# A planner's charges for VectorE, ScalarE and GpSimd instructions, in a one-core hybrid encoder step

## The chip, the core and the metric

The kernel runs on one core of a Trainium2 chip. Its engines are TensorE (PE, with weight loads shown apart as PEld), VectorE (DVE), ScalarE (ACT), GpSimd (POOL) and SyncE (SP), which here issues all DMAs. The metric is the device time of one execution in microseconds, as a median of several runs.

## The reference, cut to what matters

One inference step of a one-layer encoder, for a prompt of 256 frames and 8 streams of 16 frames (384 tokens in all), model width 2048, all in float32:

```python
mem_k, mem_v = mem @ w_xk, mem @ w_xv
proj = x @ w_in                # diff q, k, v | DeltaNet q, k, v, z, a, b | two merge gates
o_a = diff_attention(...)      # 8 heads
o_b = gated_delta_chunked(...) # 16 heads; sol = triangular_solve(I + m, rhs) for each block
mix = sigmoid(gate_a) * (o_a @ w_pa) + sigmoid(gate_b) * (o_b @ w_pb)
h1 = LN(alpha * x + mix @ w_o)
h2 = LN(alpha * h1 + cross_attention(h1, mem_k, mem_v))
y  = LN(alpha * h2 + (silu(h2 @ w_ff1) * (h2 @ w_ff3)) @ w_ff2)
```

Outputs are `y` and the new caches and states.

## The kernel before

Each large product is a *job*: 16 weight tiles of 128 x 128, streamed from HBM in halves of eight tiles (512 KB, tile `raw`). ScalarE casts a half to a high part (`wh`), VectorE subtracts to get the low part (`wl`), and TensorE adds three matmuls of 384 columns for each weight tile into one accumulator `acc`. A job is 48 matmuls, and the stream of jobs (`Kern.stream`) runs through the whole kernel: memory keys and values, the gated-DeltaNet projections with 25 of the merge gates (150 to 1000 us), differential attention (1000 to 1490), the merge products, the output product (1780 to 1915), cross attention (to 2035) and the feed-forward part (2035 to 3170).

All other work is written as generators (tasks) that are woven between the matmuls. The order of every instruction on every engine is fixed while the program is written out, by a planner, the class `Driver`. It keeps one clock for each engine. `Driver.note` (called for each instruction that is emitted) adds a charge to that engine's clock and writes down when the outputs are due: 130 ns after the end. A task gives up control with `yield` and names what it waits for; `Driver.wake` lets it go on when all of that is due, plus a pad of 60 ns, by PE's planned clock. `Driver.poll` is called after each group of three matmuls (a quantum), and steps the ready task of the best priority, again and again, until nothing may run or PE's clock has moved by a budget of 300 ns. A task is held back while VectorE's or ScalarE's planned clock is ahead of PE's by more than its limit:

```python
ahead = max(self.clk["DVE"], self.clk["ACT"]) - self.clk["PE"]
if w is None or w > self.clk["PE"] or ahead > t.lim: continue
```

`Driver.until` blocks the stream itself: it polls, and where nothing can run, moves PE's planned clock on. `Driver.due` looks an operand up by tile and offset, and where that address was never written, by the tile's latest write.

In the gated-DeltaNet stage the heads go by in pairs (`HB` = 2), a block of ten jobs for each: three convolution jobs for each head, a gate job for each head and two z jobs of the pair before. Four lanes of tasks run beside them: `conv_silu` (evacuation, convolution taps on ScalarE and GpSimd, result `kq` or `vT`), `stage1` (priority 3, limit 1500; ends with the tile `vr`), `solve_lane` (priority 8, limit 900) and two `stage2_lane`s (priority 4, limit 1500; each head ends with `y`). `solve_lane` takes pair after pair: when stage 1 of both heads is done it loads the factors, runs 156 steps of the 64-row solve with 22 of the 16-row one in between, all single VectorE instructions on `sol_u`, gives up control after every fourth big step, and stores the result, which stage 2 loads as `uz`. A step works on 1 to 63 columns:

```python
for j in range(n - 1):
    for c in range(j // nsp + 1):
        nc.vector.scalar_tensor_tensor(out=u[:, c, j + 1:], in0=m(j), scalar=u[:, c, j:j + 1], in1=u[:, c, j + 1:], ...)
```

with `n`, `nsp` = 64, 16 for the big solve and 16, 8 for the small one. A convolution job of head h waits (`until`) for the end of stage 2 of head h - 6, a z job for that of head h - 5. After the last pair's convolutions come its two z jobs and seven gate jobs; the stage then waits for all its lanes.

Of the kernel before, what the change touches and what calls it, by code (L numbers as in the profile page):

```python
# [12 lines left out]
ALU = mybir.AluOpType  # L13
# [124 lines left out]
class Driver:  # L138
# [26 lines left out]
    def note(self, kind, op, a, k):  # L165
        aps = [v for v in list(a) + list(k.values()) if isinstance(v, bass.AP)]
        assert not any(v.name in self.dead for v in aps), (op, [v.name for v in aps])
        out = k.get("out")
        if out is None:
            out = aps[0]  # L170
        outs = [out] + ([k["accum_out"]] if k.get("accum_out") is not None else [])
        ins = [v for v in aps if not any(v is o for o in outs)]
        free = lambda v: v.size() // v.shape[0] if callable(getattr(v, "size", None)) else int(np.prod(v.shape[1:]))
        n = int(np.prod(out.shape[1:]))
        start = max([self.clk[kind]] + [self.due(v) for v in ins] + [self.ready.get(o.name, 0.0) if self.key(o) not in self.ready else 0.0 for o in outs])
        if kind != "PE":
            start = max(start, self.clk["PE"])
        lat = 130.0
        if kind == "DMA":
            nbytes = 4 * int(np.prod(out.shape))  # L180
            self.clk["DMA"] = max(self.clk["DMA"], start) + nbytes / 380.0
            fin = self.clk["DMA"] + 2300.0
        else:
            if kind == "PE":
                m = out.shape[0]
                if ins[0].dtype == F32R:
                    cost = 3 + n * 0.4167
                elif op == "transpose":
                    cost = 110.0
                else:  # L190
                    cost = max(4 * n * 0.4167, 110.0) * (1.0 if m > 64 else 0.65 if m > 32 else 0.36)
            elif kind == "DVE":
                f = 1.04
                if op == "tensor_reduce":
                    n = int(np.prod(ins[0].shape[1:]))
                elif op == "reciprocal":
                    f = 8.3
                elif op in ("tensor_copy", "tensor_scalar_mul", "tensor_scalar_add", "tensor_scalar", "memset") and all(
                        str(v.space) == "SB" for v in aps):
                    f = 0.52  # L200
                cost = 70 + n * f
            elif kind == "ACT":
                cost = 210 + n * 0.83
            else:
                cost = 150 + n * (2.2 if op == "tensor_tensor" else 1.2)
            fin = start + cost
            self.clk[kind] = fin
        for o in outs:
            self.ready[self.key(o)] = fin + lat
            self.ready[o.name] = max(self.ready.get(o.name, 0.0), fin + lat)  # L210
        for v in aps:
            self.last[v.name] = max(self.last.get(v.name, 0.0), fin + lat)
# [1884 lines left out]
```

## Time and profile before

| | us |
|---|---|
| median of 3 runs | 3198.93 |
| lowest, highest | 3197.56, 3202.95 |
| profiled execution | 3205.78 |
| its span, first to last instruction | 3204.0 |
| PE busy in the span | 3110.1 |
| DVE, ACT, POOL busy | 1828.2, 1215.0, 534.6 |

Busy times are unions: overlapping instructions of one engine count once. Matmuls are pipelined, so a busy PE need not be at its peak, and the spacing of its matmuls says more. The line number of nearly all instructions is 115, the helper that records them, so groups are told apart by their tiles.

### The profile page before, as it was taken

Reading aid. Unit: us, or ns where it says so; the run is one execution under the profiler, and the core shown is the slowest. Engines: PE = TensorE matmul, PEld = TensorE weight load, DVE = VectorE, ACT = ScalarE, POOL = GpSimd, SP = SyncE. Lnnn points to the kernel's source line nnn. Section 1 sums busy time; section 2 is a strip of 40 time slices with the busy share of each in tenths; the row PEclk is TensorE's granted clock in tenths of the full one; section 3 lists DMA queues with packets and bytes.
Section 4 is the critical chain, followed back from the end, with each engine's and each line's share of the span. In section 5 each row is a group of like instructions: output and inputs, shape, how many; then the busy total and the mean of one; then the engine's idle time right before and its main releaser. Section 6 shows DMA issues by size and latency. Waiting matters only on the chain.

```text
span 3204.0 us, 49130 instructions
## 1 busy us (share of the span) xinstructions
PE 3110.1 (97%) x18889; PEld 3045.3 (95%) x18889; DVE 1828.2 (57%) x3785; ACT 1215.0 (38%) x2122; POOL 534.6 (17%) x760
## 2 busy tenths in 40 slices
PE   8999999999999999999999998899999999999996
PEld 8999999988999999999999997799999999999996
DVE  5476778777762444444444767955554345555445
ACT  5554544544422443333223334433332223333332
POOL 0343433423310000000000334600000000000312
PEclk9999999999999999999999999999999999999998
DMA  8455544555554555455544756233334443333442
GB/s 280 137 148 164 162 138 144 160 151 154 142 155 163 165 179 192 155 172 183 165 148 150 259 193 217 96 127 123 125 125 122 125 127 126 120 127 123 122 127 81
DMA packets 190027, 486.22 MB, mean 152 GB/s; under 512 B 42832, under 2 KB 83296, under 8 KB 185696
## 3 DMA queue, kind: packets, MB, share of 16 engines
q1 hardware_dynamic: 189792, 483.08, 47.8%
q8 instruction: 148, 2.42, 0.3%
q14 instruction: 87, 0.71, 0.1%
HBM read 444.49 MB, written 38.50 MB: 151 GB/s over the span
## 4 chain that ended last, share of the span: by engine, by line
PE 84%; DVE 7%; DMA 4%; POOL 1%; issue 1%; ACT 1%; SPq 1%; ACTq 0%; DVEq 0%; POOLq 0%
PE acc L115 79%; DVE sol_u L115 3%; DVE wl L115 2%; PE ps L115 1%; PE ch L115 1%; DVE h L115 1%; PE do L115 1%; SPq L115 1%; PE dsc L115 1%; DMA sol_u<-in_u 1%; DMA sol_ma<-scr_ma 1%; POOL h L115 1%; POOL ln_s L115 1%; PE o L115 1%; DMA uz<-scr_up 1%
## 5 line engine op out<-in xcount | busy, mean ns | idle before, releaser
L115 DVE TENSOR_TENSOR wl<-raw,wh 128x1024 fp32r<-128x1024 f32 (+2 forms) x692 | 854.3, 1235 | 778.1 <-ACT wh L115 774.3
L115 ACT CAST wh<-raw 128x1024 fp32r<-128x1024 f32 (+2 forms) x692 | 719.1, 1039 | 1507.8 <-PE acc L115 1383.2
L115 PE MATMUL acc<-xh,wh 128*128 128x384 f32 x2320 | 819.5, 353 | 0.0
L115 PE MATMUL acc<-xh,wl 128*128 128x384 f32 x2320 | 781.0, 337 | 0.0
L115 PE MATMUL acc<-xl,wh 128*128 128x384 f32 x2320 | 780.2, 336 | 0.0
L115 PE MATMUL acc<-hh,wh 128*128 128x386 f32 x1472 | 504.4, 343 | 0.0
L115 PE MATMUL acc<-hh,wl 128*128 128x386 f32 x1472 | 499.0, 339 | 4.7 <-DVE wl L115 4.7
L115 PE MATMUL acc<-hl,wh 128*128 128x386 f32 x1472 | 499.6, 339 | 2.9 <-DVE hl L115 2.9
L115 PEld LDWEIGHTS acc<-xh,wh 128*128 128x128 f32 x2320 | 439.3, 189 | 13.2 <-issue 11.4
L115 PEld LDWEIGHTS acc<-xl,wh 128*128 128x128 f32 x2320 | 439.7, 190 | 1.5
L115 PEld LDWEIGHTS acc<-xh,wl 128*128 128x128 f32 x2320 | 438.1, 189 | 0.0
L115 PEld LDWEIGHTS acc<-hl,wh 128*128 128x128 f32 x1472 | 279.2, 190 | 5.1 <-DVE hl L115 4.1
L115 PEld LDWEIGHTS acc<-hh,wl 128*128 128x128 f32 x1472 | 278.4, 189 | 5.0 <-DVE wl L115 5.0
L115 PEld LDWEIGHTS acc<-hh,wh 128*128 128x128 f32 x1472 | 278.6, 189 | 1.9 <-issue 1.2
L115 PE MATMUL acc<-fh,wh 128*128 128x384 f32 x704 | 238.3, 338 | 0.0
L115 PE MATMUL acc<-fl,wh 128*128 128x384 f32 x704 | 238.0, 338 | 0.0
L115 PE MATMUL acc<-fh,wl 128*128 128x384 f32 x704 | 238.0, 338 | 0.0
L115 POOL TENSOR_TENSOR h<-h,ln_sh 128x384 f32<-128x384 f32 x30 | 39.2, 1345 | 927.3 <-ACT ln_sh L115 927.3
L115 POOL TENSOR_TENSOR cy<-cy,tap 128x408 f32<-128x408 f32 x144 | 177.4, 1232 | 53.0 <-ACT tap L115 48.8
L115 DVE SCALAR_TENSOR_TENSOR sol_u<-sol_mb,sol_u 128x31 f32<-128x31 f32 (+30 forms) x864 | 159.6, 258 | 0.0
L115 PEld LDWEIGHTS acc<-fh,wh 128*128 128x128 f32 x704 | 131.9, 187 | 0.1
L115 PEld LDWEIGHTS acc<-fl,wh 128*128 128x128 f32 x704 | 131.9, 187 | 0.1
(305 smaller groups left out, 3999.6 us busy)
## 6 DMA issues: line engine op xcount, KB each, us to landing
raw<-in_w_ff SPq DMA_DIRECT2D x240, 512.0 KB
raw<-in_w_gdn SPq DMA_DIRECT2D x128, 512.0 KB
raw<-in_w_diff SPq DMA_DIRECT2D x96, 512.0 KB
raw<-in_w_gate SPq DMA_DIRECT2D x64, 512.0 KB
raw<-in_w_pb SPq DMA_DIRECT2D x32, 512.0 KB
raw<-in_w_pa SPq DMA_DIRECT2D x32, 512.0 KB
raw<-in_w_o SPq DMA_DIRECT2D x32, 512.0 KB
raw<-in_w_ff SPq DMA_DIRECT2D x32, 384.0 KB
```

Of the source, the lines that this page charges most:

```text
L115: r = f(*a, **k)
```

## The change

`Driver.note` charges other durations for VectorE, ScalarE and GpSimd instructions. VectorE: 165 ns + 1.04 for each column, from 70 + 1.04; 0.65 a column for copies and the like within SBUF, from 0.52; the reciprocal's 8.3 a column goes. ScalarE: 150 + 0.87 a column, from 210 + 0.83, and 150 more where a sum is accumulated. GpSimd: a pow is 370 + 180 a column, another `tensor_tensor` 350 + 2.3 (both were 150 + 2.2), and the rest 200 + 1.2, from 150 + 1.2. The charges for PE and DMA stay. Every instruction stays; the order in which they are written out on each engine may differ.

```diff
                 if op == "tensor_reduce":
                     n = int(np.prod(ins[0].shape[1:]))
-                elif op == "reciprocal":
-                    f = 8.3
                 elif op in ("tensor_copy", "tensor_scalar_mul", "tensor_scalar_add", "tensor_scalar", "memset") and all(
                         str(v.space) == "SB" for v in aps):
-                    f = 0.52
-                cost = 70 + n * f
+                    f = 0.65
+                cost = 165 + n * f
             elif kind == "ACT":
-                cost = 210 + n * 0.83
+                cost = 150 + n * 0.87 + (150 if k.get("accum_out") is not None else 0)
+            elif k.get("op") == ALU.pow:
+                cost = 370 + 180 * n
             else:
-                cost = 150 + n * (2.2 if op == "tensor_tensor" else 1.2)
+                cost = 350 + n * 2.3 if op == "tensor_tensor" else 200 + n * 1.2
```

## Rows read from the trace of the kernel before

**Rows 1.** Busy by stretch (length; PE, PEld, DVE, ACT, POOL; PE clock; DMA; GB/s).

```profile
150.00:1000.00 850.00, 818.20 (x5183) 792.54 (x5182) 620.55 (x2050) 398.10 (x910) 289.14 (x498) 0.99 0.52 153
...
1900.00:2100.00 200.00, 174.24 (x1107) 158.61 (x1107) 161.77 (x254) 85.64 (x161) 95.29 (x80) 0.95 0.46 159
2100.00:3170.00 1070.00, 1070.00 (x6057) 1069.73 (x6057) 531.81 (x720) 316.97 (x358) 44.40 (x30) 1.00 0.39 122
```

**Rows 2.** Waits of PE, 150 to 1000 us (total, times, longest).

```profile
PE ps L115 <- DVE kq L115: 12.0, 7, 3.5
PE ch L115 <- DMA uz<-scr_up: 6.8, 5, 2.5
PE dtr L115 <- DVE lam L115: 4.4, 1, 4.4
```

**Rows 3.** Timeline of VectorE, 633 to 645 us (start, us, instruction; count last).

```profile
634.60 7.62 DVE L115 SCALAR_TENSOR_TENSOR sol_u<-sol_mb,sol_u 128x14 f32<-128x14 f32 x36
...
643.28 0.61 DVE L115 SCALAR_TENSOR_TENSOR kq<-pad,cy 128x256 f32<-128x256 f32 x2
```

**Rows 4.** Timeline of PE, 636 to 648 us.

```profile
639.97 0.33 PE L115 MATMUL acc<-xl,wh 128*128 128x384 f32 x1
640.14 0.34 PE L115 MATMUL acc<-xh,wl 128*128 128x384 f32 x1
643.75 0.71 PE L115 MATMUL ps<-cst_all,kq 128*128 128x128 f32 x3 [3.27 <-DVE kq L115]
...
644.58 0.52 PE L115 MATMUL acc<-xl,wh 128*128 128x384 f32 x1
644.90 0.52 PE L115 MATMUL acc<-xh,wl 128*128 128x384 f32 x1
```

**Rows 5.** Groups by shape (busy us, mean ns | idle before, releaser).

```profile
L115 DVE TENSOR_TENSOR wl<-raw,wh 128x1024 fp32r<-128x1024 f32 x656 | 820.0, 1250 | 769.3 <-ACT wh L115 768.8
...
L115 ACT CAST wh<-raw 128x1024 fp32r<-128x1024 f32 x656 | 689.8, 1051 | 1434.3 <-PE acc L115 1313.7 <-issue 95.8 <-ACT dtt L115 5.5
...
L115 POOL TENSOR_TENSOR cy<-cy,tap 128x408 f32<-128x408 f32 x144 | 177.4, 1232 | 53.0 <-ACT tap L115 48.8
...
L115 POOL TENSOR_TENSOR cols<-ssk,half 128x3 f32<-128x3 f32 x16 | 15.0, 935 | 24.7 <-DVE ssk L115 24.4
```

**Rows 6.** Stretches of the eight solves, instructions on `sol_u` alone (DVE busy, count).

```profile
188.00:273.00 85.00, 40.38 (x178) 0.98 0.41 128
297.00:368.00 71.00, 30.62 (x178) 1.00 0.40 126
400.00:464.00 64.00, 32.65 (x178) 1.00 0.42 122
484.00:556.00 72.00, 33.69 (x178) 0.98 0.45 144
575.00:650.00 75.00, 36.60 (x178) 0.98 0.45 138
673.00:747.00 74.00, 37.12 (x178) 0.98 0.44 137
776.00:851.00 75.00, 35.14 (x178) 1.00 0.44 136
881.00:930.00 49.00, 28.79 (x178) 1.00 0.44 135
```

**Rows 7.** The fifth stretch: instructions on `wl` (PE, PEld, DVE), then all.

```profile
575.00:650.00 75.00, 36.17 (x106) 20.29 (x106) 16.70 (x14) 0.98 0.45 138
...
575.00:650.00 75.00, 70.52 (x462) 67.42 (x461) 67.12 (x242) 39.49 (x100) 32.55 (x54) 0.98 0.45 138
```

**Rows 8.** Instructions of two tiles (ns min/median/max, first and last start).

```profile
L115 DVE TENSOR_TENSOR vr<-ps,cols x16: 545/554/558, 137.1 to 867.8; 128x384 f32<-128x384 f32 x16
...
L115 DVE SCALAR_TENSOR_TENSOR y<-o,gng,zg x16: 603/611/622, 327.5 to 978.9; 128x384 f32<-128x384 f32 x16
```

**Rows 9.** Timeline of VectorE, 372 to 378 us.

```profile
374.99 0.63 DVE L115 SCALAR_TENSOR_TENSOR kq<-pad,cy 128x256 f32<-128x256 f32 x2 [1.54 <-ACT pad L115]
```

## Prediction

> **What bounds the kernel now.** I read the busy time by stretch first [rows 1]. TensorE is the bound: from 2100 to 3170 us it is busy in all of 1070 us, and what the planner does there can win nothing. Only two stretches have slack: the gated-DeltaNet stage, 150 to 1000 us, where PE is busy 818.2 of 850 us (31.8 idle), and 1900 to 2100 us (normalisation and cross attention, 25.8 idle). The waits of PE in the first stretch come next [rows 2]: the largest are on `kq` (12.0 us in 7 waits), on the solved matrix `uz` (6.8 us) and on `lam` (4.4 us, once). The timeline shows how a wait on `kq` arises [rows 3, 4]: VectorE runs 36 solve steps from 634.60 on for 7.62 us, and only at 643.28 the `kq` for which PE has stood still for 3.27 us. TensorE then issues every 0.32 us instead of every 0.17 us, the lower of its two clock levels, so a long wait costs more than itself; the mean granted clock of the stretch, 0.99, allows at most about 8.5 us for that.
>
> So the stage is bound by TensorE, with VectorE (620.6 us busy of 850) close behind, and PE's stops there come from an order that expected VectorE to be further along.
>
> **What the change does to the charges.** No instruction is added or removed; every effect goes by the order that `Driver` writes out. Old charge, new charge and measured mean [rows 5]: `wl` of 1024 columns 70 + 1065 = 1135, then 165 + 1065 = 1230, measured 1250 ns; `wh` 1060, then 1041, measured 1051; GpSimd add of 408 columns 1048, then 1288, measured 1232; GpSimd pow of 3 columns 157, then 910, measured 935. ScalarE hardly moves. The extra 150 ns for `accum_out`, the reciprocal without its 8.3 (at most two or three columns each) and the 0.65 for copies within SBUF shift single tasks by tenths of a microsecond; I cost them at nothing, since the waits in rows 2 do not name them. If that cover is gone, one such chain is late by under 1 us for each head, 16 us at the very most and in either direction.
>
> The term that counts is the triangular solve: 178 VectorE steps for each pair of heads, 8 pairs, 1424 in all. Their column counts follow from `solve`: 3760 elements in 156 big steps, 148 in 22 small ones. Old charge for a pair: 178 x 70 + 1.04 x 3908 = 16.5 us. New: 178 x 165 + 1.04 x 3908 = 33.4 us. Measured: the eight busy times of rows 6 add up to 275.0, 34.4 us for a pair. So the new charge is right in occupancy and the old was half of it.
>
> [...]
>
> **Gain: PE's stops.** With VectorE's real backlog in its clock, the planner puts `kq`'s transposes, `vr`'s and `uz`'s matmuls behind more streaming matmuls. Of the 31.8 us idle, 4.4 us on `lam` is no matter of charges; the rest is 27.4, and with some 6 us of lower clock 33. I take 28 us. From 1900 to 2100 us much is chains with nothing else to run; I take 3 us of 25.8. The tail after 3170 is one chain: 0. Bounds of the gain: 0 and 45 us.
>
> **Loss: the solve gets slower in the order.** `solve_lane` runs at the lowest priority of its stage (8) and only while VectorE and ScalarE are planned at most 900 ns ahead of PE (`lim`). Doubling its charge doubles what each step fills of that allowance. All eight solves have 178 steps in windows of 85, 71, 64, 72, 75, 74, 75 and 49 us [rows 6]. In the fifth, VectorE has 242 instructions [rows 7]: 178 steps, 14 `wl` (one for every eighth group of three matmuls) and 50 others. Old charges: 16.5 + 15.9 + about 10.5 = 43 us, which is 0.57 of the 75 us. New: 33.4 + 17.2 + about 15 = 66 us, 0.87. The same window therefore holds the new plan only if the gate lets VectorE be planned 0.87 full, where it has been 0.57.
>
> How full can it get? The first solve answers. There every address of `sol_u` is new to the planner, so each step is charged from the tile's latest write plus 130 ns: 16.5 + 178 x 0.13 = 39.6 us, plus about 31 us for others (estimated at the fifth window's 26.4 us in 75, stretched to 85), 70.6 of 85 us = 0.83, with steps that cost about what the new ones cost. I take 0.865, between that 0.83 and the 0.87 to 0.9 at which nothing would change. The others take 32/75 = 0.43, so a later solve needs 33.4 / (0.865 - 0.43) = 77 us (83 at 0.83, 71 at 0.90) instead of 72 on average. The first has (33.4 + 23.1) / 0.435 = 130 us; TensorE comes to wait for it, which frees VectorE, and I take 125 instead of 85.
>
> The lane is a chain: solve, store, load of the next pair, solve. Between the windows of rows 6 lie 19 to 32 us; I take 21 us, near the least, where the next factors have long been there. The last solve then starts at 188 + 125 + 6 x 77 + 7 x 21 = 922 us; now it is about 881, 14 us after its pair's first part ends at 867.8 [rows 8]: the lane has no lateness left there now, and would have then. From its start to the last `y` at 978.9 [rows 8] it now takes 98 us. PE's other work (two z jobs and seven gates) would end near 979 - 28 = 951, after which nothing competes, so I take 40 us for the last solve, 8 for its store and load and 35 for the chain behind it: 922 + 83 = 1005, against 979. That is +26 us, with the stops that vanish already in it. In between, `conv_job` of heads 6 and 7 waits for the end of heads 0 and 1: the first `y` is at 327.5 [rows 8], the convolution of head 6 reaches VectorE at 374.99 [rows 9], some 20 us after its job begins, so about 28 us of slack meet 40 us of delay. TensorE stops for some 12 us there, which is not on the path as long as the last chain ends later.
>
> **Sum.** The profiled execution took 3205.8 us (span 3204.0). 3205.8 + 26 - 3 = 3228.8; it lies 6.9 us above the median of 3198.9, so the forecast on the median's scale is 3222 us.
>
> **Rivals.** *A, the lane keeps up* (0.33): planned occupancy 0.90 or more, because bigger steps leave a bigger reserve on VectorE while small matmuls push PE's clock ahead. Then T = 70, the first solve 110: last start 865, end 865 + 50 + 49 = 964, 15 us earlier than now, with the 3 us from cross attention 3181 us; a lane with no lateness at all gives 3171. It decides from about 74 us for a solve on, since each microsecond there counts six times. For it: 0.83 is already reached with holes; against it: the fifth window has 0.57. *B, the forecast* (0.45): 3222, from 3200 at T = 74 to 3250 at T = 84 with the first solve at 140, where the formula gives +83 us, of which I keep about 50 since waiting TensorE lets the lane run. *C, the lane starves* (0.10): occupancy rises to only 0.70, T = 33.4 / 0.27 = 124 us; every block then waits in `conv_job`; with the lane quick in each wait I reckon some 18 us for each of six blocks, about 3305. *D, the order hardly changes* (0.12): PE's own charges, untouched, set most of the order, and small gains and losses cancel: 3199 within 10 us.
>
> **How the numbers follow.** A measurement of this kernel can tell about 0.2% (6.4 us) from no change. Faster: 0.31 of A and 0.04 of D, 0.35. Same: 0.02 of A, 0.05 of B, 0.06 of D, 0.13. Slower: 0.40 of B, 0.10 of C, 0.02 of D, 0.52. The range goes from 3168 (below it a lane without lateness and nearly all idle time gone, 0.09) to 3285 (above it most of C, 0.09). B alone would be 3200 to 3250. Both signs hold much of the chance, and the point is B's.
>
> **What would show it.** Right: no run of over 20 solve steps between two `wl`, PE's waits on `kq` under 3 us together, and a first solve of over 110 us; windows of 75 us or more for the solves after it, the last solve starting after 900 us, and PE idle between about 950 and the end of the stage. Wrong: windows of 70 us or less, or a last solve that still starts 14 us after its pair's first part; then the gain is all that is left and A holds. PE stops of tens of microseconds ahead of a convolution job would show C. Unchanged waits on `kq` would show D. From 2100 to 3170 us nothing should move by more than 1 us.

## The result and the profile after

The changed kernel takes 3269.92 us (median of 6 runs, 3267.16 to 3273.27) against 3199.68 us before, a ratio of 1.022 [1.0209, 1.0231]: 70 us slower. The forecast was 23 us slower. Its profiled span is 3271.5 us.

Where the time went, by the windows view of the kernel after (length; PE, PEld, DVE, ACT, POOL busy with counts; PE clock; DMA share; GB/s):

```profile
150.00:1060.00 910.00, 835.56 (x5143) 806.17 (x5142) 625.82 (x2049) 396.82 (x909) 285.70 (x496) 0.95 0.48 142
...
1970.00:2170.00 200.00, 175.63 (x1106) 162.12 (x1105) 161.74 (x254) 85.34 (x160) 89.34 (x79) 0.92 0.46 160
2170.00:3240.00 1070.00, 1070.00 (x6057) 1069.73 (x6056) 530.38 (x719) 316.74 (x357) 44.43 (x30) 1.00 0.39 122
```

The last two lines answer the last two of [rows 1]: nearly the same busy times, 70 us later. All of the difference lies in the DeltaNet stage. TensorE's first matmul behind that stage starts at 1052.88 us instead of 986.05, and from there to the end the two traces agree within about 1 us. In the stage TensorE is idle for 74.4 us where it was idle for 31.8 [rows 1]: +42.6 of the +66.8 us. The other 24 us are in busy time. The granted clock is 0.95 where it was 0.99, and where it is 0.50 the stream's matmuls come 0.32 us apart instead of 0.17 [rows 4]; how much of the 24 us that makes was not taken apart.

PE's waits from 150 to 1060 us (total, times, longest), the answer to [rows 2]:

```profile
PE ch L115 <- DMA uz<-scr_up: 28.2, 3, 20.3
PE o L115 <- DVE y L115: 15.4, 7, 3.0
PE ch L115 <- DVE vr L115: 7.6, 13, 1.0
PE ch L115 <- issue: 6.0, 7, 1.4
PE o L115 <- DVE sol_u L115: 5.0, 1, 5.0
```

No wait on `kq` is left in that list; it was the largest before, 12.0 us. Instead TensorE waits for what stands behind a solve: `uz` (6.8 before), then the links of the stage-2 chain, `y` and `vr`.

The stretches of the eight solves, instructions on `sol_u` alone (DVE busy, count), the answer to [rows 6]:

```profile
190.30:342.30 152.00, 43.67 (x178) 1.00 0.44 139
363.00:450.10 87.10, 36.95 (x178) 0.96 0.36 112
471.70:536.50 64.80, 36.17 (x178) 0.95 0.39 124
560.20:620.90 60.70, 32.02 (x178) 0.94 0.40 124
643.40:764.00 120.60, 40.80 (x178) 1.00 0.44 136
791.50:856.50 65.00, 36.13 (x178) 0.95 0.38 123
879.60:949.40 69.80, 28.65 (x178) 0.95 0.43 136
973.70:1019.60 45.90, 27.91 (x178) 0.80 0.34 104
```

The first and the fifth take 152 and 121 us (85 and 75 before), at a clock of 1.00: TensorE streams on while the lane creeps. Then the stream reaches a convolution job (once a z job) whose buffer needs an earlier pair's stage 2, stops, and the lane runs quickly. The first of these stops, at the convolution of head 6, on PE's timeline:

```profile
342.90 0.34 PE L115 MATMUL acc<-xh,wl 128*128 128x384 f32 x1
...
371.66 0.67 PE L115 MATMUL acc<-xh,wh 128*128 128x384 f32 x1
```

In between, for 28.8 us, no matmul of the stream starts; in the kernel before, the longest such stop in the stage is 5.2 us. TensorE is idle for 12.2 us of it, as the chain's own matmuls run there. Where TensorE stops, all instructions (same columns as the first view):

```profile
340.00:350.00 10.00, 3.48 (x20) 3.19 (x19) 3.96 (x11) 1.44 (x2) 0.00 (x0) 0.80 0.53 145
463.00:485.00 22.00, 14.29 (x123) 10.34 (x121) 16.30 (x82) 5.49 (x24) 1.14 (x3) 0.92 0.59 160
579.00:594.00 15.00, 8.04 (x97) 5.97 (x96) 14.87 (x80) 4.20 (x19) 1.53 (x2) 0.93 0.31 86
782.00:805.00 23.00, 14.63 (x127) 11.13 (x126) 17.15 (x86) 5.58 (x24) 2.04 (x7) 0.89 0.62 159
912.00:918.00 6.00, 2.98 (x31) 1.99 (x35) 6.00 (x25) 0.88 (x3) 0.00 (x0) 0.84 0.39 116
995.00:1048.00 53.00, 20.28 (x171) 15.12 (x171) 29.69 (x160) 6.99 (x31) 5.77 (x14) 0.66 0.21 59
```

Of these 129 us TensorE is idle for 65.3, in the last stretch for 32.7: nothing competes with the last chain any more, as the timeline of PE shows (start, us, instruction; in brackets the wait ahead of it):

```profile
1004.91 0.87 PE L115 MATMUL o<-cst_all,y 128*128 128x128 f32 x3 [4.95 <-DVE sol_u L115]
1026.07 0.77 PE L115 MATMUL ch<-vr,uz 128*128 128x128 f32 x2 [20.29 <-DMA uz<-scr_up]
...
1047.25 0.87 PE L115 MATMUL o<-cst_all,y 128*128 128x128 f32 x3 [2.72 <-DVE y L115]
1047.78 0.67 PE L115 MATMUL acc<-xh,wh 128*128 128x384 f32 x1
1048.24 0.52 PE L115 MATMUL acc<-xl,wh 128*128 128x384 f32 x1
1048.56 0.52 PE L115 MATMUL acc<-xh,wl 128*128 128x384 f32 x1
...
1052.88 0.56 PE L115 MATMUL dtr<-lam,cst_all 128*128 128x2 f32 x2 [2.83 <-DVE lam L115]
```

After the stop the matmuls are 0.32 us apart, at a granted clock of 0.50 (1047.5 to 1052 us), as in [rows 4], where it is 0.50 from 644 to 647 us and 1.00 again from 648 on. The two tiles of [rows 8], after:

```profile
L115 DVE TENSOR_TENSOR vr<-ps,cols x16: 539/551/558, 142.2 to 897.7; 128x384 f32<-128x384 f32 x16
L115 DVE SCALAR_TENSOR_TENSOR y<-o,gng,zg x16: 603/617/619, 371.1 to 1048.2; 128x384 f32<-128x384 f32 x16
```

Stage 1 ends at 897.7 and the last solve starts 76 us later, at 973.7; before it was 14 us.

### The profile page after: what moved, and what is told of

The parts are those of the page before. It is cut to its first block, busy times and chain, and to the rows that moved or that the text cites. A ratio compares the mean times of both kernels' runs of the same rounds, so it can differ in the third digit from the quotient of the medians.

```text
span 3271.5 us, 49139 instructions
## 1 busy us (share of the span) xinstructions
PE 3137.3 (96%) x18889; PEld 3070.5 (94%) x18889; DVE 1836.9 (56%) x3785; ACT 1214.5 (37%) x2122; POOL 526.5 (16%) x760
## 4 chain that ended last, share of the span: by engine, by line
PE 64%; DVE 2%; DMA 1%; issue 0%; ACT 0%; POOL 0%; SPq 0%; ACTq 0%; DVEq 0%; POOLq 0%
PE acc L115 61%; PE do L115 1%; PE dsc L115 1%; DVE h L115 1%; PE fb L115 0%; DMA rawx<-scr_ob 0%; DVE wl L115 0%; PE xss L115 0%; DVE ln_s L115 0%; DVE lu L115 0%; PE dtr L115 0%; PE xsp L115 0%; ACT h L115 0%; DMA raw<-in_w_xo 0%; PE st L115 0%
## 5 line engine op out<-in xcount | busy, mean ns | idle before, releaser
L115 DVE SCALAR_TENSOR_TENSOR sol_u<-sol_mb,sol_u 128x31 f32<-128x31 f32 (+30 forms) x864 | 178.0, 278 | 0.0
```

Of the source, the lines that this page charges most:

```text
L115: r = f(*a, **k)
```

## The experiments

Times are medians; each ratio is against the kernel before on the same chip, with its 95% interval. One reading is given for each kernel beside its time: the *sum* of the stretches of its eight solves, first step to last, and when the last solve starts. For the kernel before they are 556.5 us and 881.7, for the one after 665.9 us and 973.7.

**Which charges?** e1 and e3 start from after, e2 and e4 from before.

```diff
# e1, from after: solve steps at their old charge
-                cost = 165 + n * f
+                cost = (70 if str(out.name).startswith("sol_u") else 165) + n * f
# e2, from before: solve steps alone at the new charge
-                cost = 70 + n * f
+                cost = (165 if str(out.name).startswith("sol_u") else 70) + n * f
# e3, from after: ScalarE's and GpSimd's charges as before, so VectorE's alone are new
# e4, from before: ScalarE's and GpSimd's new charges, VectorE's as before
```

> The changed kernel, but the steps of the triangular solve (instructions that write sol_u) keep the old fixed part of 70 ns; all other charges are the new ones. Theory S (the doubled charge of the solve steps makes the solve lane late): the solve windows are about 70 us again, the first about 85 us, the last solve starts near 880 us, and the time is 3200 us, within 15. Theory C (the other charges, for the convolution's chain of ScalarE and GpSimd and for stage 1 and 2, delay the heads): the time stays near 3260 us, and the windows stay at 75 us and more.

3216.49, ratio 1.005 [1.0035, 1.0065]; sum 600.7, last solve at 912.1. Theory S misses, by 1.5 us in the time and by 32 us in the last solve; theory C is farther off.

> The kernel before, but the solve steps alone get the new fixed part of 165 ns. Theory S: most of the loss is there, 3250 us within 20, with a first solve of over 110 us and the last solve starting after 920 us. Theory C: 3200 us within 8, since nothing else is charged anew.

3226.07, 1.0081 [1.0066, 1.0096]; sum 607.1, last solve at 935.0. Between the ranges of the two theories.

> The new charges for VectorE alone, ScalarE and GpSimd at the old ones. Theory S: 3265 us within 12, all of the loss. Theory C: 3215 us or less, since the pow at 910 instead of 157 ns, the add at 1288 instead of 1048 ns and the accumulation at 150 ns are left out.

3226.35, 1.008 [1.0065, 1.0095]; sum 588.9, last solve at 934.8. Between the ranges again.

> The new charges for ScalarE and GpSimd alone, VectorE at the old ones. Theory S: 3200 us within 8. Theory C: 3255 us within 15. If the loss needs both together, e3 and e4 both stay below 3240 us.

3196.77, 0.9987 [0.9977, 0.9996]; sum 580.8, last solve at 894.9. Theory S's range, and with e3 the third case: the loss needs both.

The solve step's charge alone gives +26 us, and the rest of VectorE adds nothing to it (e2 and e3 are the same): that is the size of the forecast's own loss. ScalarE's and GpSimd's charges alone give -4. Together they give +70, so some 48 us arise only where both are there. Expecting effects to add up was wrong in e1, e2 and e3.

**What joins them?** ScalarE's planned clock, the second in the gate's `ahead`, is one candidate. e5 lets the solve lane's gate look at VectorE's lead alone (`Driver.idle`, which moves PE's clock on where nothing can run, still reads both); e6 and e7 give GpSimd or ScalarE its old charges; e11 gives them to GpSimd's `tensor_tensor` alone.

```diff
# e5, from after (the solve lane is the only task of priority 8)
+            lead = self.clk["DVE"] - self.clk["PE"]
-                if w is None or w > self.clk["PE"] or ahead > t.lim:
+                if w is None or w > self.clk["PE"] or (lead if t.prio == 8 else ahead) > t.lim:
# e6, from after
-            elif k.get("op") == ALU.pow:
-                cost = 370 + 180 * n
-                cost = 350 + n * 2.3 if op == "tensor_tensor" else 200 + n * 1.2
+                cost = 150 + n * (2.2 if op == "tensor_tensor" else 1.2)
# e7, from after
-                cost = 150 + n * 0.87 + (150 if k.get("accum_out") is not None else 0)
+                cost = 210 + n * 0.83
# e11, from after
-                cost = 350 + n * 2.3 if op == "tensor_tensor" else 200 + n * 1.2
+                cost = 150 + n * 2.2 if op == "tensor_tensor" else 200 + n * 1.2
```

> The changed kernel, all new charges, but the solve task (priority 8) is held back by VectorE's planned lead alone and no longer by ScalarE's. Theory G (ScalarE's planned lead, stretched by the new charges, shuts the gate for the solve): the first solve shrinks from 152 to under 110 us, the last starts before 925 us, and the time is 3215 us, within 12. Theory V (VectorE's own plan is full, so the gate is shut by VectorE): the first solve stays over 140 us and the time over 3255 us.

3217.51, 1.0048 [1.0032, 1.0065]; sum 600.9, last solve at 914.0. Theory G had it, with a first solve of 99.9 us.

> The changed kernel with GpSimd at its old charges (adds 1048 instead of 1288 ns, pow 157 instead of 910). If the 44 us that ScalarE's and GpSimd's charges add on top of VectorE's come by GpSimd (its longer adds let the next tap on ScalarE wait for its buffer, so ScalarE's clock runs ahead): 3230 us, within 10. If they come by ScalarE's own charges: 3265 us, within 10.

3239.61, 1.0114 [1.0099, 1.0129]; sum 630.7, last solve at 948.1. The first range, at its edge: most of the joint loss comes by GpSimd.

> The changed kernel with ScalarE at its old charges (no 150 ns for an accumulation, 210 instead of 150 ns fixed). If GpSimd's charges make the 44 us: 3265 us, within 12. If ScalarE's do: 3230 us, within 10.

3277.02, 1.0232 [1.0217, 1.0247]; sum 642.3, last solve at 979.4. The edge of the first range again: ScalarE's own charges do not make the loss.

> After, with GpSimd's tensor_tensor charged as before (150 + 2.2 a column); its power keeps the new charge, as do VectorE and ScalarE. With all of GpSimd at its old charges the time was 3239.6. Theory A (the adds make those 30 us: they hold the convolution's buffers, which moves ScalarE's planned clock ahead and shuts the solve lane's gate): 3235 to 3250. Rival P (the power makes them): 3262 to 3275. In between, both.

3252.12, 1.016 [1.0146, 1.0174]; sum 618.2, last solve at 953.0. Between the two ranges: the adds and the power share it.

In the changed kernel the look at ScalarE's plan holds 52 of the 70 us. GpSimd's charges make 30 of the 70 us, its adds 18. These shares overlap and do not add up: the old charge for the solve steps alone gives 53 us back as well (e1). ScalarE's own new charges make no clear difference: the medians of e7 and after lie 7 us apart, and the intervals of their ratios (1.0217 to 1.0247 and 1.0209 to 1.0231) overlap. How an add of GpSimd gets into ScalarE's planned clock I read from the code: the taps that ScalarE writes for the convolution share buffers that GpSimd's adds free, so a longer add pushes the next tap, and ScalarE's clock, ahead. That link is argued, not measured. What the gate does is in the trace after, in the first solve, for all instructions and then for `sol_u` alone:

```profile
197.20:217.00 19.80, 19.80 (x117) 19.57 (x116) 14.85 (x27) 12.98 (x28) 10.24 (x15) 1.00 0.48 146
```

```profile
197.20:217.00 19.80, 2.78 (x9) 1.00 0.48 146
```

In 19.8 us, VectorE does 9 of the 178 steps and stands idle for 5 us, with the next step at hand. Which of the two leads shut the gate there the trace does not tell; the first solve falls from 152 us to 100 in e5, and to 104 in e9 below, which takes another charge off VectorE's own plan.

**Would a quicker first solve, or a wider gate, do?** e9 tells the planner that the solve's buffers are ready, so that the first solve loses its charge for unknown addresses; e10 raises the limit.

```diff
# e9, from after
+            for tt in (u, u2):
+                for c in range(tt.shape[1]):
+                    for j in range(1, tt.shape[2]):
+                        nc.ready.setdefault(nc.key(tt[:, c, j:]), 0.0)
# e10, from after
-            ends.append(d.spawn(self.solve_lane(), prio=8, lim=900.0))
+            ends.append(d.spawn(self.solve_lane(), prio=8, lim=2500.0))
```

> After, with one thing added: the planner is told that the zeroed columns of both solve buffers are ready from the start, so that the steps of the first solve no longer carry the charge for an operand whose address it does not know; the instructions are the same. Theory F (the first solve's stretch of 152 us is lengthened by that charge, and its delay of 67 us against before is carried to the last solve): first solve 100 to 120, last solve start 935 to 955, time 3225 to 3250. Rival R (the lane is held by its gate, which lets it have a fixed share of the planned time, so that a shorter first solve is given back in later stretches): last solve start 965 or later, time 3260 to 3275.

3262.45, 1.0193 [1.0179, 1.0207]; sum 627.5, last solve at 969.1. Rival R had it.

> After, with the solve lane's limit raised from 900 to 2500 planned ns of lead; all charges are those of after. Theory G (the gate, shut by ScalarE's and VectorE's planned lead, is what holds the solves back): the stretches of the solves 1, 3 to 8 go to 50 to 75 us, last solve start before 915, time 3205 to 3240. Rival (the lane is held by what the other tasks issue, not by its gate): last solve start 955 or later, time over 3255.

3263.74, 1.0196 [1.0181, 1.0211]; sum 445.7, last solve at 942.2. Theory G had the solves, its rival the time.

In e9 the first solve falls from 152 to 104 us, and the fourth takes 132: the last starts 5 us earlier, no more. The lane's lateness is made over the stage, not by its first solve. In e10 the solves are short (54 to 62 us, the last 44), as theory G said, and the time is still 3264: theory G was wrong in that a quicker lane is always better. There stage 1 ends late (its last `vr` about 927 us), and the lane waits for it.

**Is there a lane that is too quick?** e13 joins e1 and e5; e15 makes the edit of e5 in the kernel before, and e16 makes it with VectorE's charges as before (e4). The gate then lets the solve run while its steps are charged at half of VectorE's busy time for them (16.5 of 34.4 us for a pair).

> After, with both changes that each left 16 us: the fixed part of a solve step is 70 again, and the solve lane's gate looks at VectorE's lead alone (limit 900). Theory D (two doors to one lane, and the 16 left by each is what the other door holds): solves of 45 to 70 us, last solve start 870 to 890 (behind stage 1's end), time 3185 to 3203. Rival T (a third cause, in the other charges): last solve start over 900, time 3208 to 3222.

3249.67, 1.0146 [1.0131, 1.0161]; sum 485.7, last solve at 926.0. Neither theory had it.

> Before, all charges old, with one change: the solve lane's gate looks at VectorE's lead alone. If ScalarE's part of the gate held the lane in before too, the solves fall from 49 to 85 us to 40 to 65, the last starts within 10 us of stage 1's end, and the time is 3180 to 3198. If that was no hindrance since the lane had no lateness left, 3197 to 3206; a packed VectorE then also lengthens PE's waits on kq, from 12 us to 15 to 25.

3266.16, 1.0197 [1.0182, 1.0212]; sum 397.1, last solve at 942.1. Neither: the solves fall to 47 us as the first said, and the time rises by 62.

> ScalarE's and GpSimd's charges new, VectorE's old (that was 3196.77), and the solve lane's gate looks at VectorE's lead alone. If the gate's ScalarE part still costs there: 3180 to 3193, faster than both kernels. If not: 3194 to 3203.

3272.24, 1.0217 [1.0201, 1.0234]; sum 393.1, last solve at 949.0. Neither case: slower than both kernels, as e15.

The trace of e15 shows why: one solve, the gap behind it, and PE's waits from 150 to 1060 us.

```profile
603.00:651.00 48.00, 38.07 (x243) 34.13 (x242) 46.66 (x207) 18.61 (x49) 16.82 (x33) 0.99 0.42 121
651.00:717.00 66.00, 66.00 (x405) 64.40 (x403) 30.36 (x55) 32.30 (x71) 21.60 (x33) 0.98 0.56 151
```

```profile
PE ps L115 <- DVE kq L115: 21.5, 11, 4.2
PE ch L115 <- DVE vr L115: 21.3, 20, 2.9
PE ch L115 <- DMA uz<-scr_up: 12.8, 7, 3.3
```

During the solve VectorE is busy for 46.7 of 48 us, and TensorE, which needs `kq` and `vr` from it, stands for 9.9 us (7.0 of them on these two) and does 243 matmuls, 5.1 for each us. Then VectorE has 30 us of work in 66. A pair takes 113 us from solve to solve, where the kernel before has 99.

**Pace alone, and the right price.** e17 is e15 with the limit 100 as a brake. e8, e14 and e18 start from after with the gate of e5 and charge the solve step by its spacing in the trace (see the last section), with limits of 1300, 900 and 700. e12 is e8 with nine gate jobs instead of seven kept for the stage's end.

```diff
# e17, from e15
-            ends.append(d.spawn(self.solve_lane(), prio=8, lim=900.0))
+            ends.append(d.spawn(self.solve_lane(), prio=8, lim=100.0))
# e14, from e5; e8 and e18 also set lim to 1300.0 and 700.0
-                cost = 165 + n * f
+                cost = (129 if str(out.name).startswith("sol_u") else 165) + n * f
# e12, from e8
-        for _ in range(7):
+        for _ in range(9):
```

> Before, all charges old, the solve lane's gate looks at VectorE's lead alone, and its limit is 100 instead of 900 (with 900: 3266.16, solves of 47 us in which VectorE is busy for 46.4). Theory P (what counts is the pace at which the plan lays down solve steps; without a brake VectorE is full for the whole solve and TensorE stops behind it): the low limit is the brake, solves of 58 to 78 us, PE stops of e15 mostly gone, 3185 to 3215. Rival Q (the old charges need the look at ScalarE itself, a limit does not replace it): solves under 55 us, 3235 or more.

3197.09, 0.9978 [0.9968, 0.9988]; sum 521.7, last solve at 889.3. Theory P.

> A version that follows from theory G: all new charges, but a solve step is charged with the distance at which the steps start in the trace (129 ns and 1.04 for each column) instead of its duration, its gate looks at VectorE alone, and its limit is 1300 ns. Theory G: the lane keeps up, the last solve starts before 870 us, PE's stops stay small, and the time is 3190 us, within 12. Theory V: the lane keeps up too, but with less cover, 3215 us or more.

3200.06, 0.9995 [0.9986, 1.0004]; sum 511.1, last solve at 876.5. Theory G's time; its last solve before 870 is missed.

> The run with solve steps charged by their spacing (129 + 1.04 a column) and the gate looking at VectorE alone, but with the limit 900 instead of 1300 (that run: 3200.06; with the charge 165 and limit 900: 3217.5). If the charge brought the 17 us, 3198 to 3205; if the limit, 3212 to 3220.

3185.88, 0.9948 [0.9932, 0.9965]; sum 558.7, last solve at 860.3. This is faster than both kernels, and than either case expected.

> The run with solve steps charged by their spacing and the gate looking at VectorE alone, with the limit 700 (900: 3185.88, 1300: 3200.06). If the limit has its best near 900 (faster lane: VectorE full; slower lane: late last chain), 3186 to 3200. If a smaller limit is better still, because VectorE keeps more room for kq and vr: 3175 to 3185.

3193.69, 0.997 [0.9957, 0.9983]; sum 576.2, last solve at 892.2. The first case: 900 is the best of the three limits.

> The run with solve steps charged by their spacing and the gate looking at VectorE alone with 1300 (3200.06), with one change: nine instead of seven gate jobs are kept for the end of the stage, to be issued while the last solve runs. If TensorE's idle piece at 955 to 981 us is for want of work in the last solve, two more jobs fill about half of it: last y 965 to 975, time 3183 to 3195, faster than both kernels. If it is for want of the last chain's own operands, the time stays within 3197 to 3205.

3201.66, 1.0004 [0.9995, 1.0014]; sum 514.6, last solve at 878.1. More jobs at the end bring nothing.

e17 has the old charges and no look at ScalarE, as e15, and a brake: 69 us less. So the loss of the quick lane is its pace, not the missing look. e14 against e5, where the price alone differs, is -32 us. The sum lines of four kernels over their own eight solves (PE, PEld, DVE, ACT, POOL), in the order after, before, e14, e15:

```profile
sum 665.90, PE 618.87 PEld 600.38 DVE 531.00 ACT 300.05 POOL 206.18; mean PE 77.36 PEld 75.05 DVE 66.37 ACT 37.51 POOL 25.77
```

```profile
sum 556.50, PE 530.57 PEld 510.42 DVE 494.50 ACT 268.09 POOL 194.61; mean PE 66.32 PEld 63.80 DVE 61.81 ACT 33.51 POOL 24.33
```

```profile
sum 558.60, PE 550.34 PEld 533.58 DVE 516.81 ACT 279.77 POOL 209.25; mean PE 68.79 PEld 66.70 DVE 64.60 ACT 34.97 POOL 26.16
```

```profile
sum 397.10, PE 334.00 PEld 311.58 DVE 390.27 ACT 163.70 POOL 137.25; mean PE 41.75 PEld 38.95 DVE 48.78 ACT 20.46 POOL 17.16
```

VectorE's share of the solves is 0.80 after, 0.89 before, 0.93 in e14, 0.98 in e15; TensorE's idle time in them is 47, 26, 8 and 63 us. By the sum of the eight stretches the kernels fall into three groups:

| sum of solves, us | kernels | time, us |
|---|---|---|
| 393 to 486 | e16, e15, e10, e13 | 3272, 3266, 3264, 3250 |
| 511 to 581 | e8, e12, e17, before, e14, e18, e4 | 3200, 3202, 3197, 3200, 3186, 3194, 3197 |
| 589 to 666 | e3, e1, e5, e2, e11, e9, e6, e7, after | 3226, 3216, 3218, 3226, 3252, 3262, 3240, 3277, 3270 |

Among these kernels the lane has a best pace, between some 510 and 580 us for eight solves. Below it VectorE is full and TensorE stops behind it (e15); above it the lane is late and TensorE stops for its chain (after). The pace alone is varied where only the limit differs: e15 and e17 (397 and 522 us: 3266 and 3197), and e8, e14 and e18 (511, 559, 576 us: 3200, 3186, 3194). The borders of the groups are drawn after the fact, and the sum alone does not set the time: e4 at 581 us takes 3197, e3 at 589 us 3226. The kernel before stood near the best by two errors that balanced: a fixed part of 70 ns for a step, where the spacing has 129, and a gate that also looks at ScalarE. The change raised the first past the spacing, to 165, and left the second.

What stays open: in e10 TensorE is idle for only 18 us within the solves, the rest of its loss lies between them (its longest wait, 10.3 us, is on ScalarE's `kws`), and which order there costs it was not taken apart. Nor does VectorE's share alone part the first group from the second: it is 0.94 in e13 (3250 us) and 0.95 in e8 (3200 us). Within the third group the sum orders the times only roughly.

## Why the prediction was wrong in size

**The bound and the place: right.** The planner moves nothing behind the stage; 2170 to 3240 us is busy throughout.

**The gain from PE's stops: a sign that came true, and a sum that did not.** The waits on `kq` went from 12.0 us to none that the list shows, as forecast. But PE's idle time in the stage rose from 31.8 to 74.4 us: other stops took their place. The 3 us for cross attention were 0 (idle 24.4 us in its stretch; 25.8 before).

**The price of a solve: wrong, though no term of the sum, which goes by the charge.** "The new charge is right in occupancy" took the union of busy times, 34.4 us for a pair. In a run of steps VectorE passes one every 130 to 201 ns, though each lasts 210 to 283 (medians of the kernel before, at 1 and 63 columns); at 129 + 1.04 a column a pair is 178 x 0.129 + 1.04 x 3.908 = 27.0 us, close to the 27.9 of the last solve after. e14 against e5 (3185.88 and 3217.51 us) says that the spacing, and not the length of one step, is what the planner wants here.

**The fill of the plan: the step that failed.** "How full can it get? The first solve answers" set 0.865 from VectorE's lead alone. The gate takes the larger of two leads, and ScalarE's shut it as well: e5 gives 52 us back. GpSimd's charges stand at nothing in the sum, and e6 puts them at 30 us: "ScalarE hardly moves" was true of its charges, and the adds were listed with their new price and then not followed to the gate. With VectorE's charges alone, e3, the ends come out as forecast: a first solve of 119.6 us (forecast 125), the last at 934.8 (922), the last `y` at 1007.4 (1005), the time up by 26 us (23). In between, the other six solves take 427 us (462) and the gaps 201 (147), so a part of that agreement is luck. The working has one slip of little weight: 26.4 us stretched from 75 to 85 is 29.9, not 31, and the fill 0.82, not 0.83.

**The sum for the lane.** Forecast: last solve at 922; it was 973.7. The 52 us between: the first solve 152 instead of 125 (+27), the seven gaps 163 us instead of 147 (+16), the six solves between 468 instead of 462 (+6), the start 190.3 instead of 188 (+2). The mean of the six, 78.0 against 77, was right by luck: they run from 61 to 121 us, slow where TensorE streams (the 121 us, in which it is idle for 0.0) and quicker where it stands (the other five, 61 to 87 us, idle for 3.1 to 7.0 in each). e9 shows that the first solve's own 27 us are not a cause: cut by 48 us they come back in the fourth. The end behind it was 74.5 us instead of 83.

**The stops in each block.** The prediction kept "tens of microseconds ahead of a convolution job" for rival C and let B stop once, for 12 us, off the path. TensorE stopped ahead of four of the five blocks that have such a wait, and at one z job: 32.6 us idle in the five stretches shown before the last, and at the first of them the stream of weight matmuls stood for 28.8 us, which is close to C's sign. The result is B's mechanism with a part of C's.

**Rival A** priced a lane without lateness at 3171 to 3181 us. e14 is such a lane (last solve at 860.3, forecast of A 865) and takes 3185.9, with steps charged less than in the change and the gate altered.

**Signs.** `kq` waits under 3 us, first solve over 110, last solve after 900, and TensorE idle at the stage's end: seen. "No run of over 20 solve steps between two `wl`": wrong; the last solve has 124 in a row and two earlier ones 102, since nothing streams while TensorE stands. "Later windows of 75 or more": only two of seven.

## What to carry to other kernels

A planner's charges and its brakes are tuned as one: raise the charge of a step that was too low, and a gate that had made up for it becomes a second brake, so look at every clock the gate reads before pricing the change. Charge an instruction by the spacing that a run of its kind shows on its engine, not by the length of one: here 130 ns against 210 at one column, and 32 us between e14 and e5. Here a background lane had a best pace, and lost on both sides of it: read from the solve's stretch whether the shared engine is full (0.98 busy here) or has holes with work at hand.

## What the runs showed of the hardware

In a run of solve steps VectorE starts each well before the one ahead of it ends by its record. In e15, with start and length:

```profile
604.32 0.28 DVE L115 SCALAR_TENSOR_TENSOR sol_u<-sol_ma,sol_u 128x62 f32<-128x62 f32 x1
604.52 0.23 DVE L115 SCALAR_TENSOR_TENSOR sol_u<-sol_m,sol_u 128x14 f32<-128x14 f32 x1
604.66 0.28 DVE L115 SCALAR_TENSOR_TENSOR sol_u<-sol_ma,sol_u 128x61 f32<-128x61 f32 x1
604.85 0.23 DVE L115 SCALAR_TENSOR_TENSOR sol_u<-sol_m,sol_u 128x13 f32<-128x13 f32 x1
```

The step of 62 columns lasts 0.28 us, and the next starts 0.20 us after it; of 14 columns, 0.23 and 0.14. Over all steps of the kernel before, the median spacing is 130 ns behind a step of 1 column, 145 behind 15, 161 behind 31 and 201 behind 63.
